# A two-layer retention and stick-breaking trunk on one core: the opening's products in another order, and the heads' norm statistics on the scalar engine

## The chip, the core and the metric

The kernel runs on 1 core of a Trainium2 chip. A core has TensorE for products, VectorE and ScalarE for work on whole tiles, GpSimd (POOL) for more of that, and SyncE (SP), whose queue issues all DMAs here. Matmul results land in PSUM, eight banks of 128 x 512 numbers; everything else lies in SBUF. The metric is the device time of one execution in microseconds, lower is better.

## What is computed

```python
def hybrid_layer(x, c_act, norm_g, w_ada, b_ada, w_in, w_out, pos):
    mod = c_act @ w_ada + b_ada                      # c_act = silu(c), one row
    shift, scale, gate = split(mod, 3)
    h = rms_norm(x, norm_g) * (1 + scale) + shift    # 1024 rows of 1024
    proj = h @ w_in                                  # 1024 -> 4096, eight parts of 512
    y_ret = retention(rotary(q), rotary(k), v)       # 4 heads of 128, chunks of 64
    #   ... o is normed per row and head: (o - mean) * rsqrt(var + EPS)
    y_ret = y_ret * silu(g_r)
    y_sb = stick_breaking(q_s, k_s, v_s) * silu(g_s) # 8 heads of 64
    return x + gate * (concat(y_ret, y_sb) @ w_out)
# two layers, then a last rms_norm; all in fp32
```

## The kernel before, in words

**Precision.** Each large product is three fp16 products: an operand is split into a high and a low part (`hh`, `hl` of h; `w[:, 0]`, `w[:, 1]` of a weight), and high x high, high x low and low x high are summed in one bank. High parts are made by ScalarE, low parts by VectorE.

**Who sets the order.** Every engine takes its instructions strictly in order. That order is made when the program is built: `Flow` runs generators ("streams"), one for each chain of steps, and keeps a clock of estimated prices for each engine (`price`). A stream yields what it waits for (tiles or named marks, room in a pool, an engine, a slack in ns); the planner lets the stream of lowest rank go on whose needs are met at TensorE's planned time, and if none is, moves on to the first that can. So a changed price or a changed yield can move instructions anywhere in the program. On the chip each instruction then waits by semaphores for its real operands.

**The opening.** `start` loads eight blocks of x (`xt`), the scale and shift columns of the first layer's `w_ada` (`ada`, for k = 0 to 7 one tile each of scale and shift) and the first weight group (`wst`). For each column k of h the sums `c_act @ w_ada` are needed. For k below 4 `first_direct` makes them on TensorE: eight fp32 products of 128x1 for each of scale and shift, into one column of the bank `sums`; this is a *group* below. For k from 4 on the products are made by VectorE (scale, `first_scale`) or by ScalarE and GpSimd (shift, `first_shift`), and TensorE only sums over partitions with a row of ones. `summed` adds the bias on VectorE (`s` and `sh` in the rows). x is normed (`first_norm`) and transposed by TensorE (`turned`, `xt<-ident,xt`, 32 for each half of the rows), copied to `xT` by VectorE and ScalarE in turn, and `kept` makes h from it: GpSimd writes `h`, ScalarE `hh`, VectorE `hl`. The first projections (`begin`, `acc<-hh,w` and `acc<-hl,w`) run column by column as h comes. `awake` is the stream of lowest rank: wherever the planner has nothing else for TensorE, it puts in an idle product (`idle<-own`) that nobody reads.

**The layers.** Then per layer four pairs of stick-breaking heads (P) and four retention heads (R) are projected and worked through, in the order of `ORDER`; eight row blocks for each. `retain` takes one block of one retention head: rotation, the state (`rst`), scores, the output `po` in PSUM, its norm and gate, and a transpose by DMA into `y`. At most three blocks are in flight (`roomr`). `out_project` multiplies `y` by `w_out`; its results are added to x. The second layer ends with the last norm.

Of the kernel before, what the change touches and what calls it, by code (L numbers as in the profile page):

```python
# [13 lines left out]
F32 = mybir.dt.float32  # L14
AF = mybir.ActivationFunctionType
ALU = mybir.AluOpType
PSUM = bass.MemoryType.PSUM
DRAM = bass.MemoryType.DRAM

P = 128  # L20
# [6 lines left out]
EPS = 1e-6  # L27
# [5 lines left out]
DS = 1.0 / WS  # L33
AS = 256.0
VS = 16.0
RS = 2.0 ** -10


def retention_constants():
    f = np.float32  # L40
    lg = np.log1p(-(f(2.0) ** (f(-5.0) - np.arange(4, dtype=f)))).astype(f)
    i = np.arange(P, dtype=f)
    m, c = i[:, None], i[None, :]
    same = (i[:, None] // 64) == (i[None, :] // 64)
    later = (c // 64) > (m // 64)
    mask = np.zeros((P, 4, P), f)
    qdec = np.exp((i[:, None] + f(1.0)) * lg[None, :]).astype(np.float64)
    for h in range(4):
        dec = np.exp((np.abs(c - m) - (c + 1)).astype(np.float64) * lg[h])
        mask[:, h] = np.where(same | later, dec * np.exp((m - 127.0) * lg[h]), 0.0) * RS  # L50
    kdec = np.exp((f(127.0) - i)[:, None] * lg[None, :]).astype(f)
    bdec = [float(np.exp(f(P) * lg[h])) for h in range(4)]


    cols = np.concatenate([kdec * f(DS * VS), EPS * P * (VS * RS / qdec) ** 2], 1).astype(f)
    return mask, cols, bdec


# [9 lines left out]


MASK, COLS, BDEC = retention_constants()  # L70


# [27 lines left out]
class Flow:  # L100
# [32 lines left out]
    def price(self, kind, name, outs, ins):  # L133
        n = outs[0].free_size()
        if kind == "pe":
            if name == "transpose":
                return 109 if ins[0].dtype == F32 else 64
            if ins[0].dtype == F32:
                return 210 if n < 16 else 61 + n * 4 / 2.4
            rows, cols = ins[0].shape[0], outs[0].shape[0]  # L140
            turn = 97 * (self.shape not in (None, (rows, cols)))
            self.shape = rows, cols
            if 64 in (rows, cols):
                return turn + max(1.5 + n / 4.8, 27)
            return turn + max(2.5 + n / 2.4, 56)
        if kind == "act":
            scales = sum(1 for a in ins[1:] if a.free_size() == 1)
            return n / 1.2 + (51 if ins[0].space == PSUM else 93) + 93 * scales
        if kind == "dve":
            n = max([n] + [a.free_size() for a in ins])  # L150
            if name == "tensor_tensor_scan":
                return 68 + 2.083 * n
            if name == "bn_stats":
                return 170 + n / 0.96
            if name == "bn_aggr":
                return 217
            scales = sum(1 for a in ins if a.free_size() == 1)
            return (n + 65) / 0.96 + 62 * scales
        if kind == "pool":
            if name == "memset":  # L160
                return 36 + 0.84 * n
            if name == "tensor_scalar" and n > 1:
                return 200 + 0.9 * n
            if n == 1:
                return 500 if outs[0].tensor.name.startswith(("rrs", "rs", "r_")) else 268
            return 20 + 3.1 * n if n < 512 else 150 + 2.1 * n
        if name == "dma_start_transpose":
            return 225 + 0.88 * n
        size = outs[0].free_nbytes() * outs[0].shape[0]
        run = 4 * outs[0].shape[-1]  # L170
        return size / run * (8 + 0.037 * run) / 16
# [121 lines left out]
def trunk(ctx: ExitStack, tc, x, c, norm_g, w_ada, b_ada, w_in, w_out, final_g,  # L293
          rot, rmask, rcols, out):
    nc = tc.nc
    flow = Flow()
    pe, act, dve, pool, sp = (Engine(flow, k, e) for k, e in (
        ("pe", nc.tensor), ("act", nc.scalar), ("dve", nc.vector), ("pool", nc.gpsimd), ("dma", nc.sync)))
# [3 lines left out]
    wk = Slots(flow, ctx.enter_context(tc.tile_pool(name="wk", bufs=2)), 2)  # L302
# [16 lines left out]
    def bank(name, tag="g", bufs=5):  # L319
        return ps.tile([P, 512], F32, tag=tag, bufs=bufs, name=name)  # L320
# [5 lines left out]
    def apart(tile):  # L326

        flow.big.add(tile.tensor.name)
        return tile
# [5 lines left out]
    own = const.tile([P, S], BF16, name="own")  # L335
# [25 lines left out]
    rcols_sb = const.tile([P, 8], F32, name="rcols_sb")  # L361
# [95 lines left out]
    sums = apart(bank("sums", "av", 1))  # L457

    def summed(pt, ks, third):

        m = (shs, s1s)[third][0]
        kk = slice(ks[0], ks[-1] + 1)
        dve.tensor_add(m[:, kk], pt[:, 0:len(ks)], bg[:, third * 8:third * 8 + 8][:, kk])
        if third:
            dve.tensor_mul(m[:, kk], m[:, kk], bg[:, 48:56][:, kk])
        for k in ks:
            flow.mark(("first", third, k))

    def first_columns(acc, ks, third):
# [5 lines left out]
        yield [pt]  # L475
        summed(pt, ks, third)

    def first_direct(ks, st, third):

        pt = sums[:, 8 * third + ks[0]:8 * third + ks[-1] + 1]  # L480
        yield ()
        for i in range(len(ks)):
            for r in range(NK):
                pe.matmul(pt[:, i:i + 1], st[:, r, i * P:(i + 1) * P], c_act[:, r:r + 1],
                          start=(r == 0), stop=(r == NK - 1))
        yield [pt]
        summed(pt, ks, third)

# [478 lines left out]
    def retain(l, h, b, acc, state, turn, mask):  # L967
# [3 lines left out]
        gs = wk.tile([P, P], F32, tag="rg", bufs=3, name="rg")  # L971
        act.activation(gs, acc[:, 384:512], AF.Sigmoid, scale=DS)
        kdec = rcols_sb[:, h:h + 1]
# [8 lines left out]
        roomrot.n += 1  # L982
        dve.scalar_tensor_tensor(out=vd[:, 1], in0=acc[:, 256:384], scalar=kdec, in1=vd[:, 0],
                                 op0=ALU.mult, op1=ALU.subtract)
        dve.scalar_tensor_tensor(out=gs, in0=acc[:, 384:512], scalar=DS, in1=gs,
                                 op0=ALU.mult, op1=ALU.mult)
        pool.tensor_tensor(out=t1[:, 0::2], in0=t1[:, 0::2], in1=t2[:, 1::2], op=ALU.subtract)
        pool.tensor_tensor(out=t1[:, 1::2], in0=t1[:, 1::2], in1=t2[:, 0::2], op=ALU.add)
        turned = t1.rearrange("p a f -> p (a f)")
# [11 lines left out]
        def product(o, ah, al, bh, bl, start=True, stop=True):  # L1001
            pe.matmul(o, ah, bh, start=start, stop=False)
            pe.matmul(o, ah, bl, start=False, stop=False)
            pe.matmul(o, al, bh, start=False, stop=stop)

        old, old16 = state[0] or (None, None)
        if b < NT - 1:
            yield [vd, rk], roomg.has(), "pe"
            roomg.n -= 1
            pkv = bank("psc")  # L1010
            product(pkv[:, 0:P], rk[:, 0, P:], rk[:, 1, P:], vd[:, 0], vd[:, 1])
            new = wk.tile([P, P], F32, tag="rst", bufs=3, name="rst")
            yield [pkv]
            if b == 0:
                dve.tensor_copy(new, pkv[:, 0:P])
            else:
                dve.scalar_tensor_tensor(out=new, in0=old, scalar=BDEC[h], in1=pkv[:, 0:P],
                                         op0=ALU.mult, op1=ALU.add)
            roomg.n += 1
            new16 = wk.tile([P, 2, P], F16, tag="rs16", bufs=3, name="rs16")  # L1020
            yield [new]
            act.mul(new16[:, 0], new, RS)
            yield [new16]
            dve.scalar_tensor_tensor(out=new16[:, 1], in0=new, scalar=RS, in1=new16[:, 0],
                                     op0=ALU.mult, op1=ALU.subtract)
            state[0] = new, new16
        yield [("qkT", l, h, b)], roomg.has(), "pe"
        roomg.n -= 1
        psc = bank("psc")
# [12 lines left out]
        po = bank("po")  # L1042
        if b > 0:
            product(po[:, 0:P], qkT[:, 0], qkT[:, 2], old16[:, 0], old16[:, 1], stop=False)
        product(po[:, 0:P], sm16[:, 0], sm16[:, 1], vd[:, 0], vd[:, 1], start=(b == 0))
        yield [po]
        st = wk.tile([P, 6], F32, tag="rbs", name="rbs")
        dve.bn_stats(out=st, in_=po[:, 0:P])
        mv = wk.tile([P, 2], F32, tag="rmv", name="rmv")
        dve.bn_aggr(out=mv, in_=st)  # L1050
        ve = wk.tile([P, 1], F32, tag="rve", name="rve")
        pool.tensor_tensor(out=ve, in0=mv[:, 1:2], in1=rcols_sb[:, 4 + h:5 + h], op=ALU.add)
        rs = wk.tile([P, 1], F32, tag="rrs", name="rrs")
        pool.tensor_tensor(out=rs, in0=ve, in1=nhalf[:, 0:1], op=ALU.pow)
        y0 = sm
        dve.scalar_tensor_tensor(out=y0, in0=po[:, 0:P], scalar=mv[:, 0:1], in1=gs,
                                 op0=ALU.subtract, op1=ALU.mult)
        roomg.n += 1
        if b % 2 == 0:
            yield (), roomy.has()  # L1060
# [9 lines left out]
                                 op0=ALU.mult, op1=ALU.subtract)  # L1070
        flow.mark(("yt", l, h, b))
        roomr.n += 1
        if b % 2:
            yield [("yt", l, h, b - 1), ("yt", l, h, b)], None, None, LOADED
            sp.dma_start_transpose(out=y[:, h, b - 1:b + 1].rearrange("p b a q -> p (b a) q"),
                                   in_=both.rearrange("p b a e -> p (b a e)"))
# [265 lines left out]

    def awake():

        idle = bank("idle", "pj", 2)
        while True:
            yield [own]
            if ("h", 0, 0, 0) in flow.done:
                return
            pe.matmul(idle[:, 0:256], own[:, 0:P], own[:, 0:256], start=True, stop=True)  # L1350

    flow.spawn(NORM, start())
    flow.spawn(WARM, awake())
    flow.spawn(MAIN, layers())
    flow.run()
# [23 lines left out]
```

## Time and profile before

| | |
|---|---|
| median of 3 runs | 1092.58 us (1087.74 to 1222.69) |
| the profiled execution | 1092.43 us, of it the span 1090.0 us |
| TensorE busy | 1053.6 us, 97% of the span |
| VectorE / ScalarE / GpSimd busy | 879.2 / 550.7 / 247.7 us |
| DMA | 159.61 MB, mean 146 GB/s |

The span runs from the first instruction to the last. PE is TensorE, DVE VectorE, ACT ScalarE, POOL GpSimd. All compute instructions are recorded in one helper, so their line is L90 everywhere, and rows are told apart by engine, operation and tile names. Each fp32 product appears as two or more records, so that a group of eight 128x1 products is 16 records. The records of one engine overlap: the start of the next record, not the end of the last, gives the pace. The granted clock is the share of TensorE's full rate that the throttle let through.

### The profile page before, as it was taken

To read this page: it belongs to the slowest core of one execution; us is meant where nothing else is said; L and a number is where in the kernel's file an instruction comes from. 1 tells how busy PE (TensorE), PEld (TensorE's weight loads), DVE (VectorE), ACT (ScalarE), POOL (GpSimd) and SP (SyncE) were. 2 spreads that over 40 slices of the span, in tenths; PEclk is the share of its full clock that TensorE was granted. 3 is DMA by queue.
4 is the path that set the end of the run, shared out by engine and by line. 5 is a ranking of instruction groups with operands and counts; after the bars stand their busy time and mean duration, and the time that the engine had idled before them with its cause. 6 is when DMAs were issued, how large, how long until landed. Compare 5 with 4: busy or idle time off the path is not lost. (4 is left out here: it accounts for less than half of the span.)

```text
span 1090.0 us, 18647 instructions
## 1 busy us (share of the span) xinstructions
PE 1053.6 (97%) x6472; PEld 525.4 (48%) x6472; DVE 879.2 (81%) x1673; ACT 550.7 (51%) x1263; POOL 247.7 (23%) x557
## 2 busy tenths in 40 slices
PE   6989999999999999999899999999999999999996
PEld 5834444444455544544445444444454445545443
DVE  2488998899899968999455788976899789999544
ACT  3566556535454455481444555544645555555112
POOL 2382330133014202320100034000133013343002
PEclk8699999999999999999999999999999999999999
DMA  9915756766686746367581565665735473647664
GB/s 291 241 50 137 157 112 150 181 137 162 156 201 150 155 91 143 69 172 180 171 239 61 120 142 104 138 159 120 158 78 139 85 153 71 150 82 175 198 238 144
DMA packets 343901, 159.61 MB, mean 146 GB/s; under 512 B 228032, under 2 KB 319232, under 8 KB 343808
## 3 DMA queue, kind: packets, MB, share of 16 engines
q1 hardware_dynamic: 343808, 158.44, 60.3%
q8 instruction: 50, 0.82, 0.3%
q14 instruction: 43, 0.35, 0.1%
HBM read 92.32 MB, written 11.53 MB: 95 GB/s over the span
## 5 line engine op out<-in xcount | busy, mean ns | idle before, releaser
L90 PE MATMUL acc<-hh,w 128*128 128x512 f16 x1024 | 323.0, 381 | 0.7 <-DVE q L90 0.6
L90 PE MATMUL acc<-w,hh 128*128 128x512 f16 x1024 | 305.0, 379 | 0.0
L90 PEld LDWEIGHTS <-w 128*128 128x128 f16 x1536 | 145.7, 99 | 179.7 <-issue 21.3
L90 PE MATMUL acc<-hl,w 128*128 128x512 f16 x512 | 195.0, 381 | 0.8 <-DVE hl L90 0.8
L90 PE MATMUL acc<-w,hl 128*128 128x512 f16 x512 | 194.0, 379 | 0.0
L90 POOL TENSOR_TENSOR t<-t,t 128x128 f32<-128x128 f32 (+1 forms) x192 | 130.9, 696 | 232.6 <-DVE t L90 196.4
L90 PE MATMUL acc<-w,y 128*128 128x512 f16 (+1 forms) x792 | 170.8, 374 | 3.3 <-ACT y L90 3.1
L90 PEld LDWEIGHTS <-hh 128*128 128x128 f16 x1024 | 92.3, 98 | 96.8 <-issue 10.8
L90 DVE TENSOR_TENSOR_SCAN keep<-keep,own 128x640 f32<-128x640 f32 (+3 forms) x60 | 114.3, 1911 | 18.8 <-ACT keep L90 18.7
L90 PEld LDWEIGHTS <-y 128*128 128x128 f16 x792 | 76.5, 98 | 91.2 <-ACT y L90 3.6
L90 DVE SCALAR_TENSOR_TENSOR w<-wst,w 128x512 f16<-128x512 f32 x160 | 110.8, 714 | 8.2 <-ACT w L90 7.9
L90 ACT ACTIVATE w<-wst 128x512 f16<-128x512 f32 x160 | 96.5, 635 | 15.2 <-DMA wst<-in_w_in_dram 11.9
L90 ACT CAST t<-t 128x256 f16<-128x256 f32 (+1 forms) x128 | 44.3, 352 | 88.5 <-POOL t L90 53.3
L90 ACT CAST keep<-beta 128x640 f16<-128x640 f32 (+3 forms) x60 | 53.0, 885 | 63.5 <-DVE beta L90 63.2
L90 PEld LDWEIGHTS <-hl 128*128 128x128 f16 x512 | 50.1, 98 | 60.4
L90 ACT ACTIVATE keep<-z 128x512 f32<-128x512 f32 (+3 forms) x120 | 63.7, 531 | 20.6 <-PE z L90 20.1
L90 DVE TENSOR_TENSOR keep<-beta,keep 128x640 f16<-128x640 f32 (+3 forms) x60 | 61.2, 1024 | 7.5 <-ACT keep L90 7.5
L90 PE MATMUL z<-k,q 64*128 64x512 f16 (+3 forms) x576 | 64.6, 328 | 1.3 <-ACT beta L90 0.5
L90 ACT ACTIVATE beta<-z 128x512 f32<-128x512 f32 (+4 forms) x120 | 64.3, 536 | 0.0
L90 DVE SCALAR_TENSOR_TENSOR beta<-beta,keep 128x639 f32<-128x639 f32 (+3 forms) x60 | 62.5, 1047 | 0.0
L90 DVE TENSOR_TENSOR t<-acc,turn 128x256 f32<-128x256 f32 x128 | 47.9, 415 | 17.2 <-ACT vd L90 16.2
L90 DVE TENSOR_TENSOR_SCAN both<-both,own 128x128 f32<-128x128 f32 (+3 forms) x64 | 55.1, 869 | 7.2 <-ACT both L90 7.2
(122 smaller groups left out, 1307.4 us busy)
## 6 DMA issues: line engine op xcount, KB each, us to landing
wst<-in_w_in_dram SPq DMA_DIRECT2D x128, 256.0 KB, 3.5
wst<-in_w_ada_dram SPq DMA_DIRECT2D x64, 256.0 KB, 3.1
ada<-in_w_ada_dram SPq DMA_DIRECT2D x16, 512.0 KB, 6.5
wst<-in_w_out_dram SPq DMA_DIRECT2D x32, 256.0 KB, 3.4
x<-xh SPq DMA_DIRECT2D x24, 256.0 KB, 2.6
xt<-in_x_dram SPq DMA_DIRECT2D x8, 512.0 KB, 5.3
turn<-in_rot_dram SPq DMA_DIRECT2D x64, 64.0 KB, 2.3
xt<-x SPq DMA_DIRECT2D x8, 512.0 KB, 4.4
```

The lines of the kernel that those rows point to most:

```text
L90: real(*args, **kw)
```

## The change

Four edits. `first_direct` yields before each group for the mark of the group before it plus 600 ns, so that two groups no longer follow each other while another stream can go on. The idle products write into the second half of the bank `sums`, instead of a bank of the projections, and may be put in until h of the last column of the second half is there, instead of the first column of the first half. In `retain` the mean and the sum of squares of a block of `po` are made by two ScalarE passes with an accumulator, instead of `bn_stats` and `bn_aggr` on VectorE; factors of 128 go into the constants, and the planner's price has 186 ns more for an accumulator. A block's state waits, in the planner, for the mark of the block before.

```diff
-    cols = np.concatenate([kdec * f(DS * VS), EPS * P * (VS * RS / qdec) ** 2], 1).astype(f)
+    cols = np.concatenate([kdec * f(DS * VS), EPS * P * P * (VS * RS / qdec) ** 2], 1).astype(f)
...
-            return n / 1.2 + (51 if ins[0].space == PSUM else 93) + 93 * scales
+            read = 186 * (len(outs) > 1)
+            return n / 1.2 + (51 if ins[0].space == PSUM else 93) + 93 * scales + read
...
+    direct = []
     def first_direct(ks, st, third):
         pt = sums[:, 8 * third + ks[0]:8 * third + ks[-1] + 1]
-        yield ()
+        yield direct[-1:], None, None, 600
+        direct.append(("direct", third, ks[0]))
         for i in range(len(ks)):
             for r in range(NK):
                 pe.matmul(pt[:, i:i + 1], st[:, r, i * P:(i + 1) * P], c_act[:, r:r + 1],
                           start=(r == 0), stop=(r == NK - 1))
+        flow.mark(direct[-1])
...
-        dve.scalar_tensor_tensor(out=gs, in0=acc[:, 384:512], scalar=DS, in1=gs,
+        dve.scalar_tensor_tensor(out=gs, in0=acc[:, 384:512], scalar=DS * P ** 0.5, in1=gs,
...
+        if b > 0:
+            yield [("state", l, h, b - 1)]
...
+            flow.mark(("state", l, h, b))
...
-        st = wk.tile([P, 6], F32, tag="rbs", name="rbs")
-        dve.bn_stats(out=st, in_=po[:, 0:P])
-        mv = wk.tile([P, 2], F32, tag="rmv", name="rmv")
-        dve.bn_aggr(out=mv, in_=st)
+        junk = turned[:, P:]
+        nm = wk.tile([P, 1], F32, tag="rmv", name="rmv")
+        act.activation(junk, po[:, 0:P], AF.Identity, scale=-1.0 / P, accum_out=nm)
+        yield [nm]
+        sq = wk.tile([P, 1], F32, tag="rbs", name="rbs")
+        act.activation(junk, po[:, 0:P], AF.Square, bias=nm[:, 0:1], accum_out=sq)
+        yield [sq]
...
-        idle = bank("idle", "pj", 2)
+        idle = sums[:, 256:512]
         while True:
             yield [own]
-            if ("h", 0, 0, 0) in flow.done:
+            if ("h", 0, 1, 7) in flow.done:
                 return
```

**TensorE, from the first group of sums to the second pair.** `sums<-c_act,ada` x8 is one group, `xt<-ident,xt` a transpose, `own` the operand of an idle product (which now writes `sums`). Before:

```order
L90 MATMUL sums<-c_act,ada 128x1 x16
L90 LDWEIGHTS own
L90 MATMUL idle<-own 128x256
...
L90 MATMUL xt<-ident,xt 128x128 x32
L90 MATMUL sums<-c_act,ada 128x1 x16
L90 LDWEIGHTS w
L90 MATMUL acc<-hh,w 128x512
```

Now:

```order
L90 MATMUL sums<-c_act,ada 128x1 x8
L90 LDWEIGHTS own
L90 MATMUL sums<-own 128x256
...
L90 MATMUL sums<-c_act,ada 128x1 x8
L90 MATMUL xt<-ident,xt 128x128 x32
L90 MATMUL sums<-c_act,ada 128x1 x8
L90 LDWEIGHTS own
L90 MATMUL sums<-own 128x256
...
L90 MATMUL sums<-c_act,ada 128x1 x8
L90 LDWEIGHTS w
L90 MATMUL acc<-hh,w 128x512
```

Five idle products stand between the first two groups and four between the third and the fourth, where the groups followed each other. Later on the third pair, too, has six projections between its groups, the second transposes stand ahead of the fourth pair instead of behind it, and six idle products stand ahead of column 6's sums; idle products are 52 in all, from 39.

**VectorE, in the same place.** `s` and `sh` are the additions to the sums of scale and shift, `st` and `mv` the statistics of x, `w` a weight's low part, `hl` that of h. Before:

```order
L90 TENSOR_TENSOR sh_109<-sums,bg 128x1
L90 SCALAR_TENSOR_TENSOR w<-wst,w 128x512
L90 TENSOR_TENSOR hl<-h_305,hh 128x512
L90 BN_STATS st<-xt 128x6 x2
L90 BN_AGGR mv<-st 128x2
...
L90 TENSOR_TENSOR s_111<-sums,bg 128x1
L90 TENSOR_TENSOR s_111<-s_111,bg 128x1
L90 TENSOR_TENSOR sh_109<-sums,bg 128x1
```

Now:

```order
L90 TENSOR_TENSOR sh_109<-sums,bg 128x1
L90 TENSOR_TENSOR hl<-h_306,hh 128x512
L90 BN_STATS st<-xt 128x6 x2
L90 BN_AGGR mv<-st 128x2
L90 SCALAR_TENSOR_TENSOR w<-wst,w 128x512
L90 TENSOR_TENSOR s_111<-sums,bg 128x1
L90 TENSOR_TENSOR s_111<-s_111,bg 128x1
```

The addition for scale of column 1 has moved ahead of the second block's statistics, but stands behind the low part of h, the first statistics and the weight's low part. The fourth idle product after the third group waits for it by a semaphore.

**The statistics of a retention block.** VectorE before, `po` being the block's output in PSUM and `rg` its gate:

```order
L90 BN_STATS rbs<-po 128x6
L90 BN_AGGR rmv<-rbs 128x2
L90 SCALAR_TENSOR_TENSOR t_1060<-po,rmv,rg 128x128
L90 SCALAR_TENSOR_TENSOR rst<-rst,psc 128x128
L90 TENSOR_TENSOR t_1235<-acc,turn 128x256
```

ScalarE now:

```order
L90 ACTIVATE t_1165,rmv<-po 128x128
L90 ACTIVATE rs_1341<-rst 128x128
L90 ACTIVATE t_1165,rbs<-po,rmv 128x128
L90 ACTIVATE rg<-acc 128x128
L90 ACTIVATE vd<-acc,rcols_sb 128x128
```

The two statistics have left VectorE, and two passes over `po` stand on ScalarE among its other work, 64 times each.

## Rows read from the trace of the kernel before

**Rows 1.** Busy time by stretches: stretch, length, engines' busy us (records), PEclk, DMA share, GB/s.

```profile
18.07:24.90 6.83, 6.83 (x34) 6.77 (x34) 1.71 (x4) 0.92 (x2) 0.00 (x0) 0.50 0.89 289
31.72:35.14 3.42, 3.42 (x12) 1.77 (x10) 1.54 (x4) 3.38 (x4) 2.35 (x4) 0.50 1.16 294
38.55:52.20 13.65, 13.65 (x62) 12.45 (x61) 3.98 (x9) 4.83 (x7) 3.79 (x4) 0.50 0.95 241
...
24.90:52.20 27.30, 26.89 (x153) 23.07 (x152) 11.13 (x25) 14.23 (x21) 9.83 (x16) 0.69 1.04 268
```

**Rows 2.** TensorE in order of time: start us, length us, what, records, idle before.

```profile
15.86 4.81 PE L90 MATMUL sums<-c_act,ada 128*128 128x1 f32 x32
...
20.91 5.61 PE L90 MATMUL xt<-ident,xt 128*128 128x128 f32 x32
26.93 3.29 PE L90 MATMUL sums<-c_act,ada 128*128 128x1 f32 x28 [0.41 <-DVE sh L90]
...
34.46 3.96 PE L90 MATMUL sums<-c_act,ada 128*128 128x1 f32 x32
...
40.56 6.82 PE L90 MATMUL sums<-c_act,ada 128*128 128x1 f32 x32
47.24 6.10 PE L90 MATMUL xt<-ident,xt 128*128 128x128 f32 x32
```

**Rows 3.** The same view in short windows, for the pace of each kind.

```profile
14.99 0.93 PE L90 MATMUL idle<-own 128*128 128x256 bf16 x7
...
25.15 1.15 PE L90 MATMUL xt<-ident,xt 128*128 128x128 f32 x9
...
40.84 6.33 PE L90 MATMUL sums<-c_act,ada 128*128 128x1 f32 x29
...
53.61 0.59 PE L90 MATMUL acc<-hh,w 128*128 128x512 f16 x2
```

**Rows 4.** VectorE in order of time, 26 to 31 us, and GpSimd's h.

```profile
26.12 0.69 DVE L90 COPY xT<-xt 128x512 f32<-128x512 f32 x1 [0.18 <-PE xt L90]
26.73 0.15 DVE L90 TENSOR_TENSOR sh<-sums,bg 128x1 f32<-128x1 f32 x1
26.79 0.68 DVE L90 SCALAR_TENSOR_TENSOR w<-wst,w 128x512 f16<-128x512 f32 x1
28.15 0.69 DVE L90 TENSOR_TENSOR hl<-h,hh 128x512 f16<-128x512 f32 x1 [0.68 <-POOL h L90]
28.75 1.28 DVE L90 BATCH_NORM_STATS2 st<-xt 128x6 f32<-128x512 f32 x2
30.07 0.21 DVE L90 BATCH_NORM_AGGREGATE mv<-st 128x2 f32<-128x12 f32 x1
...
26.99 1.13 POOL L90 TENSOR_SCALAR h<-xT,s,sh 128x512 f32<-128x512 f32 x1 [12.92 <-DVE sh L90]
```

**Rows 5.** Busy time by stretches, late opening and all that follows.

```profile
62.70:80.00 17.30, 13.01 (x66) 6.24 (x65) 15.52 (x42) 8.06 (x21) 13.03 (x21) 1.00 0.11 32
...
93.00:1082.00 989.00, 974.45 (x6050) 470.78 (x6048) 825.76 (x1552) 499.80 (x1167) 203.59 (x474) 1.00 0.61 144
```

**Rows 6.** Order of time: a wait of TensorE, and one of GpSimd.

```profile
78.41 0.38 PE L90 MATMUL sums<-ones,ada 128*128 128x1 f32 x2 [1.50 <-POOL ada L90]
...
67.11 0.90 POOL L90 TENSOR_SCALAR h<-xT,s,sh 128x512 f32<-128x512 f32 x1 [3.67 <-DVE sh L90]
```

**Rows 7.** DMA issues on the page: tile, count, KB each, us to landing.

```profile
ada<-in_w_ada_dram SPq DMA_DIRECT2D x16, 512.0 KB, 6.5
```

**Rows 8.** Groups by shape: records, busy us, mean ns, idle before, by what.

```profile
L90 DVE BATCH_NORM_STATS2 rbs<-po 128x6 f32<-128x128 f32 x64 | 18.3, 287 | 3.3 <-PE po L90 3.1
L90 ACT ACTIVATE rg<-acc 128x128 f32<-128x128 f32 x64 | 17.6, 275 | 28.6 <-PE acc L90 28.6
L90 DVE BATCH_NORM_AGGREGATE rmv<-rbs 128x2 f32<-128x6 f32 x64 | 11.6, 182 | 2.2
...
L90 ACT ACTIVATION_READ_ACCUMULATOR junk<-xt 128x1 f32 x22 | 4.1, 187 | 0.0
```

More of the change, by code (lines that the diff above doesn't have):

```diff
@@ L1046, in retain @@
         yield [po]
-        st = wk.tile([P, 6], F32, tag="rbs", name="rbs")
-        dve.bn_stats(out=st, in_=po[:, 0:P])
-        mv = wk.tile([P, 2], F32, tag="rmv", name="rmv")
-        dve.bn_aggr(out=mv, in_=st)
+        junk = turned[:, P:]
[5 more added lines that the diff above has]
+        yield [sq]
         ve = wk.tile([P, 1], F32, tag="rve", name="rve")
-        pool.tensor_tensor(out=ve, in0=mv[:, 1:2], in1=rcols_sb[:, 4 + h:5 + h], op=ALU.add)
+        pool.tensor_tensor(out=ve, in0=sq, in1=rcols_sb[:, 4 + h:5 + h], op=ALU.add)
         rs = wk.tile([P, 1], F32, tag="rrs", name="rrs")
@@ L1055, in retain @@
         y0 = sm
-        dve.scalar_tensor_tensor(out=y0, in0=po[:, 0:P], scalar=mv[:, 0:1], in1=gs,
-                                 op0=ALU.subtract, op1=ALU.mult)
+        dve.scalar_tensor_tensor(out=y0, in0=po[:, 0:P], scalar=nm[:, 0:1], in1=gs,
+                                 op0=ALU.add, op1=ALU.mult)
         roomg.n += 1
@@ L1343, in awake @@
     def awake():
-        idle = bank("idle", "pj", 2)
+        idle = sums[:, 256:512]
         while True:
             yield [own]
-            if ("h", 0, 0, 0) in flow.done:
+            if ("h", 0, 1, 7) in flow.done:
                 return
-            pe.matmul(idle[:, 0:256], own[:, 0:P], own[:, 0:256], start=True, stop=True)
+            pe.matmul(idle, own[:, 0:P], own[:, 0:256], start=True, stop=True)
     flow.spawn(NORM, start())
```

## The prediction

> **What bounds the kernel now.** I read first the busy time by stretches, then TensorE's order of time in the opening, then VectorE's and GpSimd's, and last the rest of the run as one stretch. From 93 us to 1082 us TensorE is busy 974.45 of 989.00 us, at full clock [rows 5]: its products are the bound, and all its waits there together are 14.5 us. So whatever TensorE loses before 93 us moves the end by about as much, and nothing else moves it far.
>
> The opening is different. The engine runs without a break from 18.07 to 24.90 and from 38.55 to 52.20, yet the granted clock is 0.50 there, and again from 31.72 to 35.14 [rows 1]. 0.50 is the lower of the two levels, 1.2 GHz; 1.00 is 2.4 GHz. What TensorE did before each fall is in [rows 2]: a block of the products that form the modulation sums (128x1, two records each), begun at 15.86, 26.93 and, after 34.46, again at 40.56. It rose again while transposes ran (20.91 and 47.24) or long projections. Over 24.90 to 52.20 the mean clock is 0.69 [rows 1], so 62% of that time was at the lower level.
>
> One product of the sums costs by record (3.29 - 0.25) / 27 = 0.113 us at the upper level [rows 2] and (6.33 - 0.35) / 28 = 0.214 at the lower [rows 3], and a group of eight products, 16 records, 1.8 or 3.4 us. A transpose is (1.15 - 0.27) / 8 = 0.11, so 32 are 3.5 us; an idle product 0.11; a projection 0.59 - 0.38 = 0.21, six of them 1.3 us [rows 3]. All these double at the lower level.
>
> Around the clock the Trainium skill (TensorE: Matmul & The Clock Gate, section "Why this matters for your kernels") says something else: what takes the full rate away is a gap without work between bursts of matmuls. Here the engine was busy 6.83 of 6.83 us from 18.07 to 24.90, with no gap before it, and had lost the clock all the same [rows 1], so the trace does not agree; by the rule the order in the opening would be no matter for the clock, and it would stay up to the end of the opening (first rival).
>
> **The change, part by part.**
>
> *Up to the end of the fourth pair of sums.* Before, eight groups, both sets of transposes and 18 projections are done at 47.24 + 6.10 = 53.3 us [rows 2]. I lay the new order out at the upper level. First group 15.86 to 17.7, three idle products to 18.0. VectorE's addition reads the bank into which idle products write, so it follows the third and the fourth follows it: 18.3; second group 18.5 to 20.3. Transposes to 23.8: no half-rate stretch here, as transposes and idle products now stand between 1.8 us groups. The addition for the shift follows the last copy, 24.4; third group to 26.2, three idle products to 26.5.
>
> Then the fourth idle product waits for an addition with much ahead of it on VectorE: from 24.4 GpSimd's 1.13 us, the low part 0.69, statistics 1.28 and 0.21, a weight's low part 0.68 [rows 4], so 28.6. TensorE stands 2.1 us there, and the sums' own products stand behind that wait. Fourth group 28.7 to 30.5, six projections 31.8, fifth group 33.6, six projections 34.9, sixth group 36.7, second transposes 40.2. The seventh group waits for an addition that now stands behind four copies of 0.69 and two low parts of 0.69, the first of which waits for 1.13 on GpSimd [rows 4]: 0.5 + 4.6 + the 0.2 of the addition after the transposes' start, near 42; it ends at 43.8, six projections 45.1, eighth group 47.0. That is the lower end: 6.3 us earlier than before.
>
> Upper end: from 24 to 30.5 only 0.4 us of other products run. In each such place the clock fell before, so I expect it to fall here. If it came back only after three quarters of the second transposes, as it did at 52.20, then 3 x 1.8 + 2 x 1.3 + 2.6 = 10.6 us of work take twice the time: 57.6, 4.3 us later than before. I take the share of the nearest rows, 62% of 10.6 = 6.6: 53.6, **+0.3 us**.
>
> *From there to 93 us.* TensorE's work stays: it waits 17.30 - 13.01 = 4.3 us from 62.70 to 80.00, mostly for GpSimd's sums of columns 5 and 6 (1.50 at 78.41) [rows 5, 6]. GpSimd itself stood 3.67 us before 67.11, for an addition behind TensorE's products for column 4 [rows 6]: these stood behind 57 projections after the transposes, now behind 42 after the eighth group, some 15 x 0.21 = 3.2 us sooner. With that, GpSimd's stall shrinks and so do TensorE's waits on it; between 0 and 4.3 I take **-3.0**. Six idle products, 6 x 0.11, are added before column 6's sums: **+0.7**, or nothing where TensorE would have waited. The DMAs stand in the same order; those of the last two blocks of x still wait for the first two groups, which end about when they did, and the two loads of column 7 now wait for the last of the second transposes, not for the fourth pair's products, and a load takes 6.5 us to land [rows 7]. Their columns are multiplied last, after 70 us, so a few us cost nothing; were they ten us late, TensorE would wait for column 7.
>
> *Statistics of the heads' norm.* VectorE loses 18.3 + 11.6 = 29.9 us in 64 blocks [rows 8]; ScalarE gains two passes over 128x128 of PSUM. The nearest row is the sigmoid of that size, 0.275, and a read of the accumulator 0.187 [rows 8]: 2 x 0.46 = 0.92 us a block, 59 us in all, on an engine busy 499.80 of 989.00 us [rows 5]. The block's chain grows by 0.92 - 0.47 = 0.45 us. Nothing on TensorE reads the normed block before the output projection, and three blocks are in flight, so the cover is the next blocks' projections. Bounds: +64 x 0.45 = 29 us if every chain lay open, -14.5 if the freed VectorE ended all waits [rows 5]. The rows are nearest to no effect: **0**. The new wait for the previous state orders only the planner's stream; the products of the state already needed that state's sum.
>
> *Constants and price.* The factors folded into the constants cost nothing: same instructions. Sum: 0.3 - 3.0 + 0.7 + 0 = -2.0 us against the profiled execution's own 1092.43 us, 0.15 us under the median of the three runs: **1090 us**.
>
> **Rivals.**
> 1. *The clock holds.* Groups are short now, and other products stand between them; for it, no more than 1.8 us of sums now stand in a row, where 3.6 stood; against it, the 6 us around 27 us with hardly any other product. Then the eighth group ends at 47.0, and TensorE's 93 - 53.3 - 4.3 = 35.4 us of work follow with few waits: 6.3 + 3.0 - 0.7 = 8.6 us earlier than the profiled execution: 1083.8. By the Trainium skill's rule named above the sum would be this one too.
> 2. *The clock stays down, slower.* Short runs of six projections between groups never bring it back: before, it came back at 35.14, with projections running, but the next time only at 52.20, deep in the transposes, with projections from 38.55 to 40.56 behind it [rows 1, 2]. Place: fourth group to second transposes; price 4.3 us later, and the 0.7 of idle products, while GpSimd's work starts as much later and the waits stay: 1097.5. It decides from the point where nearly all of that work, and not 62% of it, runs at 0.50.
> 3. *The statistics come through.* Where ScalarE is full, one chain in five of 64 reaching TensorE at 0.45 us is 6 us: 1096. Against it: no wait for the normed block among the 14.5 us.
> 4. *The idle products do nothing*: that holds in part already, as one of them waits 2.1 us, and is in my forecast.
>
> **Numbers.** Forecast 44%, first rival 28%, second 20%, third 8%. The forecast's own spread is about 4 us either way, as the clock's falls are not placed better than that: 1086 to 1094. The first rival reaches down to 1081 and the second and third up to 1099; with these ends about 2 in 10 stay outside. About 2% (22 us) is what a measurement of this kernel can tell from no change: 1070.6 and 1114.4. All cases lie inside; for a case that I don't see, 3% faster, 3% slower, 94% within.
>
> **What would show it.** The granted clock at 1.00 from 15 to about 27 us; TensorE idle near 26.5 before an idle product, released by VectorE; then 0.50 for some 10 us of 28 to 50; the eighth group's end near 53; fewer than 4.3 us of waits up to 80; from the opening's end to the last product 14 to 15 us of waits, as before. Wrong if the second transposes run wholly at 1.00 and end before 43 (rival 1), if 0.50 lasts from 28 to past 48 (rival 2), or if waits on ScalarE's statistics show on TensorE (rival 3).

## The result and the profile after

The changed kernel takes 1098.51 us (median of 8 runs, 1096.06 to 1103.0), the kernel before 1089.32 in the same count: a ratio of 1.0094, 95% interval 1.0069 to 1.012. The change made the kernel 9 us slower, where the forecast was 2 us faster. Ratios, here and below, leave out two runs of the kernel before in a slower state of the chip (1222.69 and 1116.12 us). The profiled execution of after is its shortest run, 1096.06 us with a span of 1094.3, so its trace shows 4 of the 9 us.

Busy time by stretches in the profile after; the columns are those of [rows 1]. These answer to [rows 1] and [rows 5].

```profile
20.42:23.83 3.41, 3.41 (x19) 3.41 (x18) 1.38 (x2) 0.99 (x2) 0.00 (x0) 0.50 0.86 249
30.66:40.90 10.24, 10.24 (x40) 7.31 (x39) 2.15 (x7) 5.39 (x6) 3.29 (x8) 0.50 1.19 290
24.90:52.20 27.30, 23.97 (x148) 18.85 (x146) 14.84 (x34) 17.62 (x30) 9.46 (x16) 0.81 0.93 240
62.70:80.00 17.30, 15.94 (x83) 7.83 (x81) 14.14 (x34) 8.64 (x20) 15.82 (x24) 1.00 0.06 16
93.00:1086.00 993.00, 973.35 (x6031) 468.92 (x6029) 790.27 (x1420) 536.09 (x1415) 228.52 (x474) 1.00 0.62 143
```

The opening became better: 0.81 for 0.69 over the same 27.30 us, and from 62.70 to 80.00 TensorE waits 1.4 us for 4.3. The loss is in the last row: waits of 19.7 us from 93 us on, for 14.5.

TensorE in order of time, opening of the profile after; answers to [rows 2] and [rows 6].

```profile
18.35 1.84 PE L90 MATMUL sums<-c_act,ada 128*128 128x1 f32 x16
20.06 5.36 PE L90 MATMUL xt<-ident,xt 128*128 128x128 f32 x32
25.83 1.95 PE L90 MATMUL sums<-c_act,ada 128*128 128x1 f32 x16 [0.41 <-DVE sh L90]
...
29.53 0.27 PE L90 MATMUL sums<-own 128*128 128x256 bf16 x1 [1.41 <-DVE s L90]
29.64 2.47 PE L90 MATMUL sums<-c_act,ada 128*128 128x1 f32 x16
...
34.49 3.41 PE L90 MATMUL sums<-c_act,ada 128*128 128x1 f32 x16
...
51.22 1.95 PE L90 MATMUL sums<-c_act,ada 128*128 128x1 f32 x16 [0.22 <-DVE s L90]
...
74.94 0.38 PE L90 MATMUL sums<-ones,ada 128*128 128x1 f32 x2 [1.15 <-POOL ada L90]
...
89.33 0.45 PE L90 MATMUL z<-k,q 64*128 64x128 f16 x7
```

The first product of the scores (`z`) marks the end of the opening: 89.33, and in the profile before:

```profile
92.25 0.36 PE L90 MATMUL z<-k,q 64*128 64x128 f16 x6
```

That is 2.9 us gained, with the same projections done before it. TensorE's last product ends at 1085.8 for 1081.5, so the rest of the run lost 7.2 us.

What TensorE waits for from 93 us on: what, for whom, us in total, times, longest. First before, then after.

```profile
PE psc L90 <- DMA rqkT<-t: 4.0, 3, 1.5
PE acc L90 <- ACT y L90: 3.1, 2, 1.6
PE psc L90 <- POOL t L90: 1.3, 5, 0.5
```

```profile
PE psc L90 <- POOL t L90: 7.0, 11, 1.5
PE po L90 <- DVE t L90: 2.0, 3, 0.9
PE acc L90 <- ACT y L90: 1.5, 1, 1.5
```

The new leader, `psc<-POOL t`, is the product for a block's state (line 1019): it needs the low part of the rotated key, which GpSimd makes. GpSimd's rows may explain part of it. Groups by shape, first before, then after with ScalarE's new groups; columns as in [rows 8], of which they are the other side.

```profile
L90 POOL TENSOR_TENSOR rrs<-rve,nhalf 128x1 f32<-128x1 f32 x64 | 41.7, 652 | 5.0
L90 POOL TENSOR_TENSOR rve<-rmv,rcols_sb 128x1 f32<-128x1 f32 x64 | 12.1, 190 | 123.2 <-DVE rmv L90 119.5 <-ACT keep L90 3.6
```

```profile
L90 POOL TENSOR_TENSOR rrs<-rve,nhalf 128x1 f32<-128x1 f32 x64 | 52.1, 815 | 5.0
L90 POOL TENSOR_TENSOR rve<-rbs,rcols_sb 128x1 f32<-128x1 f32 x64 | 32.7, 510 | 87.0 <-ACT t L90 87.0
...
L90 ACT ACTIVATE t<-po,rmv 128x128 f32<-128x128 f32 x64 | 23.9, 373 | 1.0
L90 ACT ACTIVATE t<-po 128x128 f32<-128x128 f32 x64 | 18.1, 283 | 30.5 <-PE po L90 29.1 <-DVE rg L90 1.3
L90 ACT ACTIVATION_READ_ACCUMULATOR t<-po 128x1 f32 x64 | 13.3, 208 | 0.0
L90 ACT ACTIVATION_READ_ACCUMULATOR t<-po,rmv 128x1 f32 x64 | 13.2, 206 | 0.0
```

Two things stand here. ScalarE's two passes are 0.28 + 0.21 + 0.37 + 0.21 = 1.07 us a block, where 0.92 was estimated. And the same GpSimd step on 128x1, `rve`, went from 0.190 to 0.510 us. My first theory grew from that: before, it began right behind VectorE's aggregate; now it begins whenever ScalarE is done, often beside a long instruction of VectorE. A place where TensorE waits behind GpSimd beside such an instruction; GpSimd, VectorE and TensorE in order of time:

```profile
993.74 2.85 POOL L90 TENSOR_TENSOR t<-t,t 128x128 f32<-128x128 f32 x2 [4.43 <-DVE t L90]
```

```profile
993.95 2.40 DVE L90 TENSOR_TENSOR_SCAN keep<-keep,own 128x1024 f32<-128x1024 f32 x1
```

```profile
999.02 0.23 PE L90 MATMUL psc<-vd,t 128*128 128x128 f16 x1 [1.49 <-POOL t L90]
```

Two GpSimd instructions of a block's rotation that take 0.87 us at 255.71 take 2.85 beside a scan of 2.40. The low part that TensorE waits for comes three instructions later, at 998.30 (`rve` itself takes 0.18 us here). The Trainium skill (SBUF — State Buffer, "SBUF: two separate sides") says that VectorE and GpSimd share a pair of ports as an exclusive lock, held for a whole instruction by whichever starts first, and that a VectorE instruction with two SBUF inputs takes it against a GpSimd one that reads SBUF. The trace agrees in the main: `rve` averages 0.20 us in the 16 places of after with no VectorE instruction of over 0.6 us beside it, and 0.61 in the other 48.

### The profile page after: what moved, and what is told of

It reads as the page before. It is cut to its first block, busy times and chain, and to the rows that moved or that the text cites. A ratio compares the mean times of both kernels' runs of the same rounds, so it can differ in the third digit from the quotient of the medians.

```text
span 1094.3 us, 18831 instructions
## 1 busy us (share of the span) xinstructions
PE 1051.3 (96%) x6485; PEld 520.3 (48%) x6485; DVE 848.4 (78%) x1545; ACT 589.7 (54%) x1519; POOL 271.9 (25%) x557
## 4 chain that ended last, share of the span: by engine, by line
PE 48%; DVE 10%; DMA 5%; issue 5%; POOL 4%; ACT 4%; SPq 1%; POOLq 0%; DVEq 0%; ACTq 0%
PE acc L90 39%; PE av L90 3%; PE z L90 3%; DVE t L90 2%; POOL t L90 2%; DMA rqkT<-t 1%; DMA ta<-keep 1%; POOL rrs L90 1%; DVE keep L90 1%; SPq L90 1%; DVE acc L90 1%; DVE w L90 1%; DVE beta L90 1%; PE psc L90 1%; PE po L90 1%
## 5 line engine op out<-in xcount | busy, mean ns | idle before, releaser
L90 POOL TENSOR_TENSOR t<-t,t 128x128 f32<-128x128 f32 (+1 forms) x192 | 126.7, 674 | 284.3 <-DVE t L90 239.3
L90 ACT CAST t<-t 128x128 f16<-128x128 f32 (+1 forms) x128 | 43.2, 350 | 77.8 <-POOL t L90 36.0
L90 ACT ACTIVATE keep<-z 128x512 f32<-128x512 f32 (+3 forms) x120 | 63.5, 529 | 10.9 <-PE z L90 10.5
L90 ACT ACTIVATE both<-z 128x128 f32<-128x128 f32 (+7 forms) x128 | 46.4, 449 | 22.3 <-PE z L90 16.7
```

Of the source, the lines that this page charges most:

```text
L90: real(*args, **kw)
```

## The experiments

Three terms need a word. The *recorded order*: the planner makes 5923 choices of a stream for the kernel before; they were written down, each stream by its name and arguments, and a kernel that follows the list takes the next stream on it that may go on. So an edit can be tried without a new order: in f_stat TensorE's 6472 records and SP's 668 DMAs stand as before to the last one.

```diff
         while self.streams:
+            s = self.next_in_order() if True else None
+            if s is None:
...
```

*The lower level* in the table is (1 - mean granted clock) x span, averaged over the runs of a kernel; 2 to 3 us of it lie behind the last product and cost nothing, and where TensorE waits for others it counts too much. *Rest* is the mean time without it. Over the 32 runs of before in the first session the times have a standard deviation of 3.7 us, the rest one of 1.3. The last columns split each profile at the first `z`, the last transpose ahead of the second layer (`pht`) and TensorE's end.

Each label is told of below.

| kernel | median (before beside it) | ratio, 95% interval | lower level | rest | opening / layer 1 / layer 2 |
|---|---|---|---|---|---|
| before | | | 10.7 to 13.2 | 1077.5 to 1078.1 | 92.2 / 504.3 / 485.0 |
| after | 1098.5 (1089.3) | 1.0094 [1.0069, 1.012] | 13.0 | 1086.0 | 89.3 / 510.5 / 486.0 |
| e1_open | 1098.2 (1091.8) | 1.0067 [1.0043, 1.0091] | 19.5 | 1079.2 | 90.3 / 513.2 / 485.9 |
| e2_stat | 1097.9 (1091.8) | 1.0055 [1.003, 1.008] | 13.3 | 1083.6 | 88.2 / 508.1 / 492.9 |
| e3_state | 1091.5 (1091.8) | 0.9994 [0.9963, 1.0025] | 12.3 | 1077.8 | 96.5 / 505.7 / 485.1 |
| e4_nostat | 1098.8 (1091.8) | 1.0062 [1.0037, 1.0087] | 19.5 | 1079.1 | 89.5 / 510.1 / 486.0 |
| f_open | 1088.9 (1091.3) | 0.9989 [0.9969, 1.0009] | 12.7 | 1076.2 | 89.3 / 505.0 / 484.4 |
| f_stat | 1093.3 (1091.3) | 1.0035 [1.0008, 1.0062] | 13.2 | 1080.9 | 92.9 / 507.9 / 486.8 |
| f_both | 1096.5 (1091.3) | 1.0066 [1.004, 1.0092] | 14.6 | 1081.3 | 89.1 / 507.5 / 485.9 |
| f_statd | 1098.4 (1091.3) | 1.008 [1.0052, 1.0108] | 17.2 | 1080.8 | 92.1 / 511.1 / 487.3 |
| f_dummy | 1128.4 (1088.7) | 1.0346 [1.0307, 1.0384] | 16.5 | 1110.4 | 92.8 / 526.1 / 498.9 |
| g_order | 1101.3 (1088.7) | 1.0112 [1.0077, 1.0146] | 10.4 | 1091.0 | 91.2 / 515.1 / 487.9 |
| n_700 | 1107.9 (1088.7) | 1.0173 [1.0132, 1.0214] | 14.4 | 1093.8 | 91.1 / 513.9 / 491.6 |
| f_busy | 1095.9 (1091.7) | 1.0036 [1.0012, 1.0061] | 14.6 | 1080.5 | 92.4 / 508.4 / 485.9 |
| w_wide | 1087.5 (1088.7) | 0.9991 [0.9966, 1.0016] | 10.4 | 1077.4 | 85.9 / 506.1 / 484.5 |
| w_120 | 1082.6 (1091.7) | 0.992 [0.9889, 0.9952] | 3.6 | 1078.7 | 82.1 / 504.8 / 484.7 |
| w_120old | 1082.7 (1093.2) | 0.9927 [0.9899, 0.9954] | 3.1 | 1079.7 | 82.4 / 504.7 / 485.3 |

**The edits one by one.** e1_open has only `first_direct`'s wait and the idle products' new place; e2_stat only the statistics with their constants and price; e3_state only the state's mark; e4_nostat is the changed kernel less the statistics. Their diffs are the pieces of the change's own. One thing goes astray in the parting: the accumulator's price also moves the opening, whose own norm uses accumulators. With it the changed kernel has 52 idle products, without it e1_open, e4_nostat and f_open have 47; f_both has the 52.

> The kernel before with the opening's two edits alone (first_direct's wait, idle products in the bank of sums until the last column of h). Statistics theory (the loss comes from the norm statistics on ScalarE, the opening gains the 2.9 us by which its first score product came earlier in the profile after, 89.3 for 92.2): 1086, waits of TensorE after 93 us about 14 us as before. Opening theory (the one profile shows a good clock; in most runs the opening is lost at 0.50, and the rest pays): 1094 or more. Order theory (any new order of the planner costs waits later on): 1094 or more, with waits after 93 us at 19 us.

> The kernel before with the statistics on ScalarE alone (two passes with an accumulator, the factors of 128, the price of the accumulator). Statistics theory: GpSimd's two small steps behind the statistics now begin when ScalarE is done, not right behind VectorE's aggregate; they then stand beside VectorE's long instructions (0.51 us for 0.19, 0.82 for 0.65 on average), the low part of the next block's key is queued behind them, and TensorE's state products wait: 1089 + 7 to 12 = 1096 to 1101, waits for GpSimd's t 5 us or more. Order theory (the state's wait in the planner does it): 1089 within 2. Opening theory: 1089 within 2.

> The kernel before with the planner's wait for the previous block's state alone. Statistics theory: 1089 within 3, waits of TensorE after 93 us near 14 us. Order theory: 1094 or more, and waits for GpSimd's t or the rotated keys' transposes at 5 us or more.

> The changed kernel with the statistics back on VectorE (constants and price too), so opening and the state's wait stay. Statistics theory: 1086, waits after 93 us at 14 us, VectorE's aggregate followed by GpSimd's 0.19 us step as before. Order theory: 1096 or more. Opening theory: 1094 or more.

The state's mark does nothing: e3_state's instructions are those of before, in the same order on each engine, and e4_nostat's those of e1_open. e2_stat, in an order of its own, is 6 us slower, as that theory had it. But the opening's edits alone cost 6 too, and not in the opening: that ends 1.9 us earlier, and layer 1 takes 8.9 us more. TensorE's order differs there; its last 2839 records, from 634 us on, stand again as before, and layer 2 takes about what it took. The place is the end of layer 1, TensorE in order of time and one stretch:

```profile
474.08 1.03 PE L90 MATMUL z<-k,q 64*128 64x512 f16 x7
476.35 1.17 PE L90 MATMUL z<-k,q 64*128 64x512 f16 x6 [1.23 <-DVE t L90]
478.95 1.44 PE L90 MATMUL z<-k,q 64*128 64x512 f16 x5 [1.43 <-ACT beta L90]
```

```profile
477.74:498.22 20.48, 15.95 (x77) 6.05 (x77) 18.12 (x26) 18.29 (x42) 1.38 (x4) 0.50 0.51 98
```

The last scores stand there one behind the other, with hardly anything between them, so TensorE waits for ScalarE and VectorE; and for 20.48 us the clock is at the lower level, where before it was 3.41 us:

```profile
478.87:482.28 3.41, 3.41 (x11) 0.79 (x12) 3.40 (x6) 3.41 (x11) 0.00 (x0) 0.50 0.29 84
```

By count the lower level makes up for 6.4 of the 7.7 us between the mean times: 19.5 us for 13.1. That it costs as much isn't shown, as ScalarE and VectorE are busy for 18.29 and 18.12 of these 20.48 us. In e4_nostat, the same program, the profile has it for 10.24 us there, 5.1 less by count, and layer 1 is only 3.1 shorter. Nor is it the changed kernel's place: the profile after has no lower level from 40.90 us to its last product.

**The same edits in the recorded order.** f_open follows the list once the opening is over, f_stat throughout, f_both has both edits.

> The kernel before with the opening's edits, but from the end of the opening on the streams go on in the order recorded for the kernel before, so that every engine's order after it is the one of before. Theory A (the new opening itself gains 2 to 3 us; with it the planner's clock reads other times, and it lays the end of the first layer otherwise, which cost 5 to 8 us there): 1091.8 - 2.5 = 1089, the end of the first layer within 1 us of before. Rival B (the opening's own work delays what follows, whatever the order): 1095 or more, as in the run of the opening's edits alone, 1098.

> The kernel before with the statistics on ScalarE, both passes issued where bn_stats stood, and all streams in the order recorded for the kernel before: TensorE's and SP's orders are those of before to the last instruction. Theory A (the statistics cost by themselves: GpSimd's two steps stand beside VectorE's long instructions, the next block's low part waits behind them): 1096 to 1099, waits for GpSimd's t at 4 us or more, rve above 0.4 us on average. Rival B (the planner's new order cost it): 1089 to 1093, waits as before.

> Opening's edits and the statistics on ScalarE together, the order after the opening recorded from the kernel before. Theory A: the sum of the two runs before it, 1094 to 1096. Rival B (order alone costs): 1089.

f_open lands on 1088.9, with 1089 expected of theory A: the opening's edits gain 2.4 us by the medians (the ratio's interval takes in 1), and their loss of 6 was the new order. f_stat shows that the statistics do cost by themselves, though less than theory A said, 3.4 us of rest, with `rve` at 0.295 us, not above 0.4, and waits for GpSimd's `t` of 2.2 us, not 4. f_both came to 1096.5, a little over the 1094 to 1096 expected. But f_open and f_stat as measured add up to 1090.9, and f_both has 3.8 us of rest where they add up to 2.1: the two edits together cost more than their sum, and why is not shown.

**Is it GpSimd's stall?** f_statd adds one VectorE copy, so that `rve` follows a VectorE instruction again.

```diff
+        ss = wk.tile([P, 1], F32, tag="rsq", name="rsq")
+        dve.tensor_copy(ss, sq)
-        pool.tensor_tensor(out=ve, in0=sq, ...
+        pool.tensor_tensor(out=ve, in0=ss, ...
```

> As the run with the statistics in the recorded order, with one copy of 128x1 on VectorE between the sum of squares and GpSimd's first step, so that this step again starts right behind an instruction of VectorE and beside a short one. If GpSimd's stall beside VectorE's long instructions is what the statistics cost: rve back to about 0.2 us, and 3 us or more of the loss back. If the longer chain over ScalarE costs it: the same time or up to 3 us more, whatever rve takes.

It didn't do what it was for: `rve` averages 0.270 us for 0.295, so the stall was not taken away, and nothing came back (rest 1080.8; the median is 5 us higher, of which 4 are the lower level by count). The theory is not refuted by it, and not shown.

**ScalarE's time or the chain?** f_dummy and f_busy keep bn_stats on VectorE and give ScalarE two passes that nobody reads: f_dummy over the output `po`, f_busy over a constant in SBUF. f_busy's:

```diff
+        act.activation(junk, mask, AF.Identity, scale=-1.0 / P, accum_out=nm)
+        act.activation(junk, mask, AF.Square, accum_out=sq)
```

> The kernel before, its statistics on VectorE as they were, and beside them the two ScalarE passes over each block of the output, whose results nobody reads; all streams in the order of before. If the statistics on ScalarE cost by ScalarE's time (its other work stands later in its queue): 1094 to 1095, like the 1093.3 of the statistics in the recorded order, or a little more, as VectorE keeps its part. If they cost by the longer chain from the output to the normed block: 1091 within 1.

> The kernel before in its own order, statistics on VectorE, and for each block two ScalarE passes of 128x128 with accumulator over a constant in SBUF, which wait for nothing and whose results nobody reads: ScalarE's 59 us alone, no longer chain. If ScalarE's time costs: 2 to 4 us above before, as with the statistics themselves. If the longer chain from the output to the normed block costs: within 1 us of before.

f_dummy lost 40 us, and is no answer: its passes read the bank that bn_stats reads, they stand behind it in the trace, and ScalarE waited 108.3 us for VectorE with all its other work behind. ScalarE's group in its trace:

```profile
L90 ACT ACTIVATE t<-po 128x128 f32<-128x128 f32 x128 | 35.7, 279 | 110.4 <-DVE rbs L90 108.3
```

f_busy is the answer: 1.0036 beside f_stat's 1.0035, rest 1080.5 beside 1080.9. ScalarE's time alone is enough for what the statistics cost in the old order, with no longer chain and with `rve` at 0.192 us as before. (f_busy leaves VectorE its 30 us; a longer chain that costs, and a freed VectorE that gives as much back, are not excluded.) No single wait carries it: all waits of TensorE from the first `z` on are 17.8 us, in f_stat 18.5 and before 14.4, and the largest from 93 us on are those of before, each a little longer:

```profile
PE psc L90 <- DMA rqkT<-t: 4.7, 5, 1.5
PE acc L90 <- ACT y L90: 3.4, 2, 1.9
PE psc L90 <- POOL t L90: 2.0, 5, 0.8
```

**Is it the order?** g_order takes the changed kernel's choices, one by one, with the statistics on VectorE; n_700 is the changed kernel with one number stirred.

```diff
-        yield direct[-1:], None, None, 600
+        yield direct[-1:], None, None, 700
```

> The changed kernel's order of streams, choice by choice, with the statistics on VectorE as before (nothing of them on ScalarE). If the new order is what costs beyond the statistics: 1091 + 8.2 - 3.3 (what the statistics cost in the old order) - 0.5 = 1094 to 1096. If the order costs only with the statistics on ScalarE in it: 1088 to 1090, like the run of the opening's edits in the recorded order.

> The changed kernel with 700 ns in place of 600 in the wait between groups, a small stir of the planner. If the changed kernel's later order is a chance outcome of the planner: another order and another time, anywhere from 1089 to 1102. If the change costs in any order: 1098.5 within 2.

g_order is 12.7 us slower than before without any statistics on ScalarE, more than the 5 expected, so the order alone costs. In this order the statistics on ScalarE are even the better choice: after has 5.0 us less of rest than g_order. 100 ns in one wait took the changed kernel from 1098.5 to 1107.9 (4 runs), beyond the 1102 that was expected at most. The largest waits of g_order are those of after:

```profile
PE psc L90 <- POOL t L90: 6.3, 9, 1.4
PE po L90 <- DVE t L90: 4.3, 8, 1.2
```

The same wait for GpSimd's `t` and GpSimd's short step, in f_both and in g_order:

```profile
PE psc L90 <- POOL t L90: 3.2, 7, 0.9
...
L90 POOL TENSOR_TENSOR rve<-rbs,rcols_sb 128x1 f32<-128x1 f32 x64 | 18.0, 282 | 118.8 <-ACT t L90 118.8
...
L90 POOL TENSOR_TENSOR rve<-rmv,rcols_sb 128x1 f32<-128x1 f32 x64 | 34.8, 543 | 78.7 <-DVE rmv L90 74.6 <-ACT w L90 4.0
```

This is where the first theory comes back. The orders that lose most have the slow step and the wait together (one profile each): `rve` 0.51 us and 7.0 us of waits in after, 0.45 and 7.9 in e2_stat, 0.54 and 6.3 in g_order, 0.55 and 8.9 in n_700; f_both has 0.28 and 3.2, e1_open 0.19 and 4.6, the kernel before 0.19 and 1.3. g_order has it with the statistics on VectorE, so it hangs on the order and not on ScalarE. Whether the stall beside VectorE is how a new order costs, or only goes along with it, no run parts.

**What is the opening's clock worth?** In w_wide and w_120 (recorded order, opening's edits) and w_120old (the kernel before, its own order) each product of the sums is made with equal columns, of which the first is read.

```diff
-                pe.matmul(pt[:, i:i + 1], st[:, r, i * P:(i + 1) * P], c_act[:, r:r + 1],
-                          start=(r == 0), stop=(r == NK - 1))
...
+            c = c_act[:, r:r + 1]
+            pe.real.matmul(wide, st[:, r], c.broadcast_to([P, 120]), start=(r == 0), stop=(r == NK - 1))
```

> The opening's edits in the recorded order, and each product of the sums made with 28 equal columns in place of one, of which the first is read; the order of every engine is that of the run with one column. If the lower clock in the opening comes from products with few columns: the clock stays at 1.00 in most of 15 to 55 us, up to 7 us of the 8.5 lost to it come back less up to 0.3 us for each of eight groups, so 1083 to 1086. If columns are no matter for it: 1089 to 1092.

> The opening's edits in the recorded order, each product of the sums made with 120 equal columns in place of one. If few columns are what lowers the clock: 1.00 from 15 to 55 us, the lower level's cost in the opening from 8.5 us (one column) and 5.1 (28 columns) to under 2, and 4 to 6 us below the kernel before. If the pauses of the engine or something else in this stretch lower it: 0.50 in the same places as with 28 columns, and 0 to 2 us below before.

> The kernel before with its own opening and order, each product of the sums made with 120 equal columns in place of one. If the columns alone hold the clock: the 11.9 us that the lower level cost in the opening come back, less what the wider products and waits behind them take, 1081 to 1084, and the opening's edits add 2 us at most. If the edits are needed too (groups in a row still lower it): 0.50 again in the rows of two groups, 1087 or more.

The stretch 15 to 55 us by columns of the row format above, of f_open (1 column), w_wide (28) and w_120 (120):

```profile
15.00:55.00 40.00, 37.61 (x242) 30.87 (x241) 18.24 (x42) 22.58 (x39) 12.42 (x21) 0.80 0.91 244
```

```profile
15.00:55.00 40.00, 37.24 (x252) 29.37 (x250) 21.45 (x46) 25.63 (x49) 15.55 (x25) 0.87 1.01 269
```

```profile
15.00:55.00 40.00, 36.66 (x265) 28.29 (x265) 25.05 (x56) 27.29 (x54) 18.16 (x31) 1.00 1.03 277
```

TensorE in w_120, a group and the pauses:

```profile
14.95 1.94 PE L532 MATMUL sums<-c_act,ada 128*128 128x120 f32 x16
...
27.24 0.27 PE L90 MATMUL sums<-own 128*128 128x256 bf16 x1 [1.33 <-DVE s L90]
...
37.10 1.21 PE L90 MATMUL xt<-ident,xt 128*128 128x128 f32 x8 [0.70 <-ACT xT L90]
```

With 28 columns the lower level still comes twice and the opening ends at 85.9; the ratio, 0.9991, is no better than f_open's, and 1083 to 1086 was expected. With 120 it does not come at all, and the 4 to 6 us expected became 9. A group with 120 columns takes 1.94 us, with one 1.84 in the profile after, and the clock stays at 1.00 in the order of f_open and with much the same pauses. The opening ends at 82.1. w_120old gets the same time without the opening's edits, with two groups in a row as before: the edits add nothing once the clock holds. At 1082.6 and 1082.7 us both beat the kernel before, by 9.1 and 10.5 us, and stand some 16 below the median of the changed kernel.

## Why the prediction was wrong

**End of the eighth group, +0.3.** Right in size: 51.22 + 1.95 = 53.2, where 53.6 was forecast and before had 53.3. TensorE stood where it was said, ahead of the fourth idle product, 1.41 us at 29.53 with 2.1 predicted from 26.5, and for what was said. VectorE in order of time in the profile after, answering to [rows 4]:

```profile
26.73 0.69 DVE L90 TENSOR_TENSOR hl<-h,hh 128x512 f16<-128x512 f32 x1 [0.95 <-POOL h L90]
27.34 1.28 DVE L90 BATCH_NORM_STATS2 st<-xt 128x6 f32<-128x512 f32 x2
28.65 0.21 DVE L90 BATCH_NORM_AGGREGATE mv<-st 128x2 f32<-128x12 f32 x1
28.77 0.64 DVE L90 SCALAR_TENSOR_TENSOR w<-wst,w 128x512 f16<-128x512 f32 x1
29.33 0.15 DVE L90 TENSOR_TENSOR s<-sums,bg 128x1 f32<-128x1 f32 x1
```

The addition stands last behind the low part, the statistics and a weight's low part. 0.50 held for 10.24 us from 30.66. One claim fell: the clock was not at 1.00 up to 27 us, but at 0.50 in the first transposes, 20.42 to 23.83. By count the two stretches cost 5.1 and 1.7 us, together 6.8 for the 6.6 forecast; that the sum fits so well is in part luck.

**From there to 93 us, -3.0 and +0.7.** Right in size: the waits from 62.70 to 80.00 fell by 2.9 us, the 1.15 at 74.94 for GpSimd behind the six idle products included. With the step before, the opening was to gain 2.0 and gained 2.9. The pair of profiles flatters it, as the one before has some 15 us of the lower level by count and the one after 10, where their runs average 13; f_open's 12 runs gain 1.8 us in the mean. For the same reason the forecast, counted from that profile's 1092.43, was no gain over the median of 1089.3.

**The statistics, 0 on the path.** This step failed. It measured 3.4 us of rest in the recorded order (f_stat); together with the opening's edits, which alone gain 1.3, it is 3.8 (f_both). The prediction looked for a reader of the normed block on TensorE and found none, and took ScalarE's 59 us for covered, on an engine busy half the time [rows 5]. f_busy showed that the same time on ScalarE without any reader costs 4 us. That it does so by the casts which then stand later in ScalarE's queue is likely, and not shown. The bounds of the step, -14.5 and +29 us, had it inside; the value taken between them was wrong. What the rest was lost to inside a block, waits behind ScalarE or GpSimd's stall beside VectorE, is not settled; f_statd failed to part them. The forecast of 14 to 15 us of waits from the opening's end on fell with this step and the next: they were 19.7.

**The sum had no term for the order.** Past the opening it counted only what the diff moves. Yet the planner's later choices moved with it, and that is the larger part: of after's 8.2 us of rest (1086.0 for 1077.8), the same operations in the old order (f_both) have 3.8; the other 4.4 are the new order's. The two shares don't simply add, as in the new order the statistics on ScalarE gain. That the order costs, and not the work alone, is shown by g_order and n_700, and by the pair e1_open and f_open, 6.4 slower and 2.4 faster by the medians with the same instructions in the opening. In the trace the new order's cost shows as waits for GpSimd, 7.0 us in after and 3.2 in f_both, of 20.0 and 17.2 from the first `z` on.

**The rivals.** The third, the statistics coming through, is nearest in time (1096), but by chance: it had 6 us for a longer chain, where the statistics cost 3.4 without one being needed and the order 4.4, and the waits for the normed block that it named are not there. The first put 8.6 us on a clock that holds, 1083.8; it did not hold in the changed kernel, but where it did, in w_120 without the statistics and without the new order, the time was 1082.6. The second, slower through the clock, has its sign but not its cause: by count the changed kernel lost 13.0 us to the lower level, and the kernel before 10.7 to 13.2. By the Trainium skill (TensorE: Matmul & The Clock Gate, "Why this matters for your kernels") gaps between bursts are what costs the rate. The runs don't agree for the opening: w_120 holds 1.00 with pauses of 1.33 and 0.70 us, and f_open, in the same order and with pauses of 1.41 and 0.32, falls to 0.50 and stays there without any pause:

```profile
28.98:42.64 13.66, 13.66 (x55) 10.62 (x55) 3.63 (x9) 6.08 (x8) 4.57 (x11) 0.50 1.12 275
```

## What to carry to other kernels

Where a planner sets the order, an edit's own price and that of the order which it sets off have to be measured apart: replay the old order with the new operations, and only then judge the edit. A half idle engine is no cover by its average: passes that nobody reads cost 4 us here on an engine busy half the time. And where the clock falls in a stretch of products with one column, making the columns many is cheap to try before moving any work.

## What was not expected of the hardware

The granted clock in a stretch is not settled by the order: e3_state, instruction for instruction the kernel before, ended the opening at 96.5 us for 92.2, with 15.4 us lost to the lower level by count for 11.9. Most of the spread of the kernel before, 1084.9 to 1096.9 us in one session of 32 runs, is that: without the lower level's cost the standard deviation falls from 3.7 to 1.3 us. An fp32 product of 128x120 paces like one of 128x1 here (1.94 and 1.84 us for eight at full clock), so the columns were all but free.
